# One decoder layer on one core: x's rows loaded earlier, one convolution tap and one gate block given to VectorE, and two sums with their low parts last

## The chip, the cores and the metric

The kernel runs as one program on one core of a Trainium2 chip. A core has TensorE (PE, matrix products into PSUM), VectorE (DVE), ScalarE (ACT), GpSimd (POOL) and a sync engine (SP) whose queue here issues nearly all DMA transfers between HBM and the on-chip memory SBUF. Each engine works through its own list of instructions in order, and waits on semaphores for the others. The metric is the device time of one execution in microseconds (us), the median of several runs.

## The reference

One layer of a hybrid decoder for 1024 tokens with 1024 channels, all in float32. Cut to what matters:

```python
h = rms_norm(x, attn_norm_w)
q, k, v, u, g = split(h @ w_in)                # 1024, 1024, 1024, 2048, 2048 columns
# branch A: differential attention, 8 heads, causal, T5 relative bias
a = softmax(q1 k1 * scale + bias) v - lam * softmax(q2 k2 * scale + bias) v   # per head, q and k RMS-normed
y_a = (rms_norm(a, subln_w) * (1 - lam_init)) @ w_proj_attn
# branch B: gated causal depthwise convolution of width 31
c = causal_depthwise_conv(u_a * sigmoid(u_b), conv_w) + conv_b
y_b = silu(layer_norm(c)) @ w_proj_conv
g_a, g_b = split(sigmoid(g + gate_b))
x = x + (g_a * y_a + g_b * y_b) @ w_out
h = rms_norm(x, ffn_norm_w)
x = x + (silu(h @ w_gate) * (h @ w_up)) @ w_down
```

## The kernel before, in words

**Numbers.** Every matrix operand is split in two: a high part, which ScalarE makes by a cast (`split_hi`, line 120), and a low part, the remainder, which VectorE (`split_lo`, line 125) or in the first stage GpSimd (`low`, line 131) makes by a subtraction. A product is then three matmuls into the same PSUM bank, `mm3` at lines 168 to 170: high by high, then one low part, then the other. Names in the profile follow that: `whi`/`wlo` are a weight's two parts, `hT_hi`/`hT_lo` those of the normalised input, `ph`/`pl` those of the softmax weights, `vh`/`vl` of the values, `aTh`/`aTl` of attention's output, `mTh`/`mTl` of the merge.

**Stages**, in order of time in the profile: an opening that loads and normalises x (to about 60 us); most of the input projection with the convolution's input u (to about 300 us); attention (to about 815 us); the two output projections and the gated merge (to about 1000 us); the product with `w_out` (to about 1070 us); the channel mixer with its gate, up and down products (to the end). Three of the products are done as seven half-size block products in place of eight (lines 438 to 448), with sums of blocks as operands; the block names "11", "12", "S1" to "S4", "22" stand for those.

**Attention.** `steps` (line 1413) lists 64 steps, one per head and row block. In each step `scores` does the score products (lines 1315 and 1316, into one of three banks `sc`), VectorE adds the bias and takes the minimum (line 1317, which frees the bank), ScalarE the exponential (1322), VectorE the combination of the two softmaxes (1332). One step later `turn` transposes the result on PE (1354, bank `pT`), ScalarE and VectorE copy it as `ph` and `pl`. Then `weigh` (lines 1359 to 1369) multiplies with the values into a bank `pW`, ScalarE copies that to `ar` (1368), and `back` transposes `ar` (1374, bank `pB`). Row blocks of the last head, 7, run in the order 6, 7, 4, 5, 2, 3, 0, 1, so the last weighting of all is `(H - 1, 0)`, with two k-steps.

Between these steps PE gets filler from a generator, `fill`: for each head the projection to q and k (`q_item`, lines 815 to 870: four passes of `gemm_N` per pair of row blocks, into banks `pg`), and the 32 blocks of the gate projection (`g_item`, lines 639 to 646: one `gemm_T` of 24 matmuls with 512 columns, then ScalarE adds the gate's bias at line 644 and the SP queue stores the block). `gemm_N` (line 381) takes eight k-steps: four on each of two weight halves, each of them a pair `whi`, `wlo`.

VectorE's own filler is the depthwise convolution, `conv_taps` (585 to 614): per channel block of 128 channels one first tap on ScalarE (line 593: input times weight plus bias into `acc`), then thirty taps on VectorE (line 599), and a store of the channel to `c_d` (605), which GpSimd's queue adds to a sum `cs_d` (583). For the last four channel blocks `acc` is a single buffer in SBUF, so the first tap of one block waits until the store of the block before it has landed.

**The end of attention** (lines 1494 to 1543): `group()` takes one more gate block from `fill`, the last `turn` follows, then `early(0)` and `early(1)` load finished heads, another `group()` takes the last gate block but one, the last weighting is done, and heads 0 to 4 are loaded (`early`, 1518) and split (`early_split`, 1522) for the projection that follows. The last gate block comes after that.

**The product with `w_out`** (1826 to 1900): at its start the SP queue gets loads of the weight blocks (`wload`, 1802: four of 256 KB for each block name), of the merge's block sums (`sload`, 1806) and of x's rows (`x_rows`, 1814: four of 256 KB for each quarter of x). VectorE makes the weight sums (`wless`, 1810), and adds each finished product to x's rows in place (1895), which frees the product's bank.

**Order.** The order of instructions on each engine is not the program's. A planner with a model of the machine's times picks it when the kernel is built. What the program pins: `with after(ins):` puts each instruction made inside the block behind `ins` on the engine of `ins`; `last_of(engine)` is the last instruction of that engine that the program has made so far; `in_order()` pins all three compute engines.

Of the kernel before, what the change touches and what calls it, by code (L numbers as in the profile page):

```python
# [16 lines left out]
P = 128  # L17
# [40 lines left out]
def kernel(  # L58
# [108 lines left out]
    def mm3(o, lh, ll, rh, rl, start, stop):  # L167
        pe.matmul(o, lh, rh, start=start, stop=False)  # L168
        pe.matmul(o, lh, rl, start=False, stop=False)  # L169
        last_mm[0] = pe.matmul(o, ll, rh, start=False, stop=stop).ins  # L170
# [86 lines left out]
    def pcol(key, k=0):  # L257
        c = col[key] + k
        return pvec[:, c : c + 1]
# [121 lines left out]
    def gemm_N(o, halves, shi, slo, i):  # L381

        ts = slice(i * P, (i + 1) * P)
        for k in range(NKT):
            whi, wlo = halves[k // 4]
            mm3(o, kt(shi, k)[:, ts], kt(slo, k)[:, ts], whi[:, k % 4, :], wlo[:, k % 4, :], k == 0, k == NKT - 1)


    v_hi = [dr.tile([S, 256], F32, name=f"v_hi{j}") for j in range(4)]
    v_lo = [dr.tile([S, 256], F32, name=f"v_lo{j}") for j in range(4)]  # L390
# [194 lines left out]
    def conv_taps(c):  # L585
        acc = []

        def first_tap():
            if c < CONV_PSUM:
                acc.append(pcv[0].tile([P, S], F32, tag="acc", name=f"acc{c}", bufs=1))  # L590
            else:
                acc.append(cv.tile([P, S], F32, tag="acc", name=f"acc{c}", bufs=1))
            act.activation(acc[0][:], us[c][:], AF.Identity, bias=pcol("conv_b", c), scale=cw[:, c, CW - 1 : CW])  # L593

        def tap(t):
            def go():
                n = CW - 1 - t
                a_ = acc[0][:, n:]
                dve.scalar_tensor_tensor(a_, us[c][:, : S - n], cw[:, c, t : t + 1], a_, op0=ALU.mult, op1=ALU.add)  # L599
                if t == 0:  # L600
                    if c < CONV_PSUM:
                        done = cv.tile([P, S], F32, tag="acc", name=f"done{c}", bufs=1)
                        act.copy(done[:], acc[0][:])
                        acc[0] = done
                    nc.sync.dma_start(c_d[c][:], acc[0][:])
                    if c == 0:
                        nc.sync.dma_start(cs_d[:], acc[0][:])
                if c > 1 and t == CW // 2:
                    with after(last_of(mybir.EngineType.DVE)):
                        add_tile(c - 1)  # L610

            return go

        return [first_tap] + [tap(t) for t in range(CW - 2, -1, -1)]
# [19 lines left out]
    def u_item(c):  # L634
        w = ws.next(), ws.next()
        for sb in range(2):
            yield from u_half(c, w, sb)

    def g_item(c):
        w = ws.next()  # L640
        for sb in range(2):
            o = gemm_T(w, hT_hi, hT_lo, sb)
            sg = wp.tile([P, 512], F32, tag="sg", name=nm("sgg"), bufs=2)
            act.activation(sg[:], o[:], AF.Identity, bias=pcol("gate_b", c))
            nc.sync.dma_start(g_d[c][:, sb * 512 : (sb + 1) * 512], sg[:])
            yield


# [166 lines left out]
    def q_item(h):  # L815
        halves = [ws.next(), ws.next()]
        t = {}
        T[h] = t
        for b in (1, 0):
            raw = qkp.tile([P, 4, 256], F32, tag="qkraw", name=nm("qkraw"), bufs=2)  # L820
            ss = sm.tile([P, 16], F32, tag="ss16", name=nm("ss16"))
            for i2 in range(2):
                o = pg()
                for e in range(2):
                    gemm_N(o[:, 256 * e : 256 * (e + 1)], halves, hT_hi, hT_lo, 4 * b + 2 * i2 + e)
                act.copy(raw[:, 2 * i2 : 2 * i2 + 2, :], o[:].rearrange("p (e c) -> p e c", c=256))
                q_squares(raw, ss, (2 * i2, 2 * i2 + 1))
                if i2 == 0:
                    yield
            r = rstd_of(ss[:], 16, 1.0 / HD, fast=h > 0)  # L830
            r4 = raw[:].rearrange("p i (g d) -> p (i g) d", d=HD)
            dve.tensor_tensor(r4, r4, r.unsqueeze(2).to_broadcast([P, 16, HD]), op=ALU.mult)

            def turn_qk(z, key, b, raw):


                dma = nc.sync.dma_start
                pt = pm("pQ")
                for i in range(4):
                    pe.transpose(pt[:, i * P : (i + 1) * P], raw[:, i, z * P : (z + 1) * P], ident[:])  # L840
                w = pcol(key + "n")

                def part(j):
                    return qkp.tile([P, 512], F32R, tag=f"{key}s{j}", name=f"{key}s{j}_{h}_{b}", bufs=2 if key == "q" else 3)

                s1, s2 = part(1), part(2)
                act.activation(s1[:], pt[:], AF.Identity, scale=w)
                lo = part(3) if key == "q" else qkp.tile([P, 512], F32R, tag="klo", name=f"klo_{h}_{b}", bufs=1)
                dve.scalar_tensor_tensor(lo[:], pt[:], w, f32(s1[:]), op0=ALU.mult, op1=ALU.subtract)
                if key == "q":  # L850
                    dma(f32(s2[HD:, :]), f32(s1[HD:, :]))
                    lo2 = part(4)
                    for one, two in ((s1, s2), (lo, lo2)):
                        if one is lo:
                            dma(f32(two[HD:, :]), f32(one[HD:, :]))
                        dma(f32(two[:HD, :]), f32(one[HD:, :]))
                        dma(f32(one[HD:, :]), f32(one[:HD, :]))
                    t["q", b] = (s1, lo), (s2, lo2)
                else:
                    act.activation(s2[HD:, :], pt[HD:, :], AF.Identity, scale=w[HD:, :])  # L860
                    dma(f32(s2[:HD, :]), f32(lo[HD:, :]))
                    dma(f32(s1[HD:, :]), f32(lo[:HD, :]))
                    t["k", b] = s1, s2

            for z, key in ((1, "k"), (0, "q")):
                free = NT * (h - 1) + (0 if key == "k" and b else NT if key == "q" and not b else NT // 2)
                late.append((free if h else 0, lambda a_=(z, key, b, raw): turn_qk(*a_)))
            yield  # L870
# [467 lines left out]
    def turn(h, i):  # L1338

        b = i // 2  # L1340
        if (h, b) not in PT:
            ph = aps.tile([P, NT, 256], F32R, tag="ph", name=nm("ph"), bufs=1)
            pl = aps.tile([P, NT, 256], F32R, tag="pl", name=nm("pl"), bufs=1)
            pool.memset(f32(ph[:, 2 * b + 1, 0:P]), 0.0)
            pool.memset(f32(pl[:, 2 * b + 1, 0:P]), 0.0)
            PT[h, b] = ph, pl
        ph, pl = PT[h, b]
        e = ES.pop((h, i))
        qs = slice((i % 2) * P, (i % 2 + 1) * P)
        for k0 in range(0, i + 1, 4):  # L1350
            n = min(4, i + 1 - k0)
            pt = pm("pT")
            for k in range(n):
                pe.transpose(pt[:, k * P : (k + 1) * P], e[:, (k0 + k) * P : (k0 + k + 1) * P], ident[:])  # L1354
            src = pt[:, : n * P].rearrange("p (k q) -> p k q", q=P)
            split_hi(ph[:, k0 : k0 + n, qs], src)
            split_lo(pl[:, k0 : k0 + n, qs], src, ph[:, k0 : k0 + n, qs])

    def weigh(h, b):

        ph, pl = PT.pop((h, b))
        vh, vl = V[h]
        o = pm("pW")
        nkt = 2 * b + 2
        for k in range(nkt):
            mm3(o[:, :256], vh[:, k, :], vl[:, k, :], ph[:, k, :], pl[:, k, :], k == 0, k == nkt - 1)
        ar = aps.tile([P, 256], F32, tag="ar", name=nm("ar"), bufs=1)
        act.copy(ar[:], o[:, :256])
        return ar
# [124 lines left out]
    n = len(steps)  # L1494
    group()
    turn(*steps[-1])
    bg.until(0)
    add_tile(NKT - 1)
    qk_ctx.close()
# [16 lines left out]
    def early(h):  # L1516
        loaded[h] = aps.tile([P, S], F32, tag="E", name=f"early{h}", bufs=4)
        nc.sync.dma_start(loaded[h][:], a_d[h][:])
# [5 lines left out]

    early(0)
    early(1)
    group()
    weighs.append((n, steps[-1][:1] + (steps[-1][1] // 2,)))
    slot(n, len(late))
    early(2)  # L1530
# [295 lines left out]
    for z, (z_, b_, s_, (l, c), full) in enumerate(WSEVEN):  # L1826
        if z == 0:
            with after(last_of(mybir.EngineType.SP)):
                wload("12", (1, 0))
                x_rows(0, 0)  # L1830
                wload("S3", (0, 1))
                wload("S1", (0, 0))
                wload("S4", (1, 1))
                sload("S2")
                x_rows(1, 1)
                x_rows(0, 1)
                sload("S4")
                sload("S3")
                x_rows(1, 0)
# [328 lines left out]
```

## Time and profile before

| | |
|---|---|
| median of 3 runs | 1724.55 us (1723.59 to 1724.76) |
| the profiled execution's own time | 1723.72 us |
| its span, first to last instruction | 1721.9 us |
| TensorE's granted clock | full in all 40 slices |
| busy: VectorE, ScalarE, GpSimd | 74%, 51%, 13% of the span |
| bytes moved by DMA | 281.66 MB, 164 GB/s in the mean |

In the rows that follow, times are us from the span's start. A row of the timeline has the start, the duration, the engine, the line of the kernel, the operation, what it writes and reads, the shapes and the number of merged instructions; in brackets stands how long the engine was idle just before, and who released it. "SPq" is the SP queue, where an instruction issues a DMA. A row of the chain has start, duration and the link. Matmuls are pipelined, and their ends are modelled: the distance between two starts is the better measure of PE's pace.

### The profile page before, as it was taken

The numbers are of one execution on the slowest core, as the hardware profiler recorded it, in microseconds if no ns is written. First come the engines' busy times: TensorE is split into PE (matmuls) and PEld (weight loads), VectorE is DVE, ScalarE is ACT, GpSimd is POOL, SyncE is SP. The second block draws the span as 40 slices with busy tenths as digits, with TensorE's granted clock in tenths as the row PEclk, the third lists the DMA queues.
The fourth block names the chain that finished last, engine by engine and source line by source line (L and its number), as shares of the span: only waits on it lengthen the run. The fifth ranks groups of instructions, "written<-read, shape, count | busy, mean of one in ns | idle before, by whom it ended". The sixth has DMA issues, their size and how long they took to land.

```text
span 1721.9 us, 25846 instructions
## 1 busy us (share of the span) xinstructions
PE 1709.5 (99%) x9237; PEld 1477.1 (86%) x9237; DVE 1277.4 (74%) x2127; ACT 870.9 (51%) x1958; POOL 227.0 (13%) x216
## 2 busy tenths in 40 slices
PE   8999999999999999999999999999999999999999
PEld 7998889998998998988888878888888888888887
DVE  7676888899888987977677769966766666575544
ACT  5334335777776786866466325633333333333332
POOL 5997851000000000000000000000000000000000
PEclk9999999999999999999999999999999999999999
DMA  6333555346345344354873683244455445597663
GB/s 207 116 122 121 154 143 158 106 120 176 94 125 165 94 125 141 100 152 139 309 237 129 202 302 102 80 141 153 153 172 166 153 145 165 176 369 271 216 217 128
DMA packets 261859, 281.66 MB, mean 164 GB/s; under 512 B 17023, under 2 KB 182480, under 8 KB 261730
## 3 DMA queue, kind: packets, MB, share of 16 engines
q1 hardware_dynamic: 253632, 266.70, 48.0%
q0 software_dynamic: 6464, 10.41, 2.8%
q10 hardware_dynamic: 1634, 2.89, 0.5%
q8 instruction: 73, 1.20, 0.3%
q14 instruction: 56, 0.46, 0.1%
HBM read 181.84 MB, written 85.50 MB: 155 GB/s over the span
## 4 chain that ended last, share of the span: by engine, by line
PE 95%; DMA 2%; DVE 1%; ACT 1%; issue 0%; POOL 0%; SPq 0%; DVEq 0%; ACTq 0%
PE acc L1005 30%; PE pg L169 13%; PE pg L170 13%; PE pg L168 13%; PE acc L493 12%; PE wo L1883 3%; PE sc L1316 2%; PE sc L1315 2%; PE pT L1354 2%; PE pg L1131 1%; PE pW L168 1%; PE pW L169 1%; PE pW L170 1%; PE pQ L840 1%; DMA room<-in_w_out_dram 1%
## 5 line engine op out<-in xcount | busy, mean ns | idle before, releaser
L599 DVE SCALAR_TENSOR_TENSOR acc<-u,cw,acc 128x1023 f32<-128x1023 f32 (+14 forms) x240 | 303.6, 1265 | 19.2 <-ACT acc L593 16.7
L170 PE MATMUL pg<-whi,hT_lo 128*128 128x256 f32 x704 | 200.7, 285 | 0.0
L169 PE MATMUL pg<-wlo,hT_hi 128*128 128x256 f32 x704 | 199.8, 284 | 0.7 <-POOL wlo L131 0.7
L168 PE MATMUL pg<-whi,hT_hi 128*128 128x256 f32 x704 | 199.0, 284 | 0.0
L125 DVE TENSOR_TENSOR wlo<-draw,whi 128x1024 fp32r<-128x1024 f32 x75 | 91.8, 1224 | 86.3 <-ACT whi L120 79.5
L120 ACT CAST whi<-draw 128x1024 fp32r<-128x1024 f32 x75 | 79.1, 1055 | 129.5 <-PE acc L493 116.0
L169 PEld LDWEIGHTS pg<-wlo,hT_hi 128*128 128x128 f32 x704 | 134.1, 191 | 3.0 <-POOL wlo L131 0.9
L168 PEld LDWEIGHTS pg<-whi,hT_hi 128*128 128x128 f32 x704 | 133.8, 191 | 1.9
L170 PEld LDWEIGHTS pg<-whi,hT_lo 128*128 128x128 f32 x704 | 134.1, 190 | 1.5
L120 ACT CAST whi<-wraw 128x1024 fp32r<-128x1024 f32 x90 | 94.6, 1052 | 60.5 <-PE pg L169 27.1
L493 PE MATMUL acc<-wlo,whi 128*128 128x512 f32 x308 | 119.8, 389 | 0.0
L493 PE MATMUL acc<-whi,wlo 128*128 128x512 f32 x308 | 119.8, 389 | 0.0
L168 PE MATMUL pg<-hT_hi,whi 128*128 128x512 f32 x288 | 115.0, 399 | 0.0
L169 PE MATMUL pg<-hT_lo,whi 128*128 128x512 f32 x288 | 114.0, 396 | 0.0
L170 PE MATMUL pg<-hT_hi,wlo 128*128 128x512 f32 x288 | 113.7, 395 | 0.0
L1322 ACT ACTIVATE E<-E,mn 128x640 f32<-128x640 f32 (+7 forms) x128 | 99.3, 776 | 20.8 <-DVE mn L1317 20.6
L120 ACT CAST whi<-s 128x1024 fp32r<-128x1024 f32 x54 | 56.8, 1052 | 95.9 <-PE acc L1005 92.6
L125 DVE TENSOR_TENSOR wlo<-wraw,whi 128x1024 fp32r<-128x1024 f32 x75 | 94.3, 1260 | 14.5 <-ACT whi L120 14.3
L1005 PE MATMUL acc<-h_lo,whi 128*128 128x512 f32 x240 | 93.4, 389 | 0.0
L1005 PE MATMUL acc<-h_hi,whi 128*128 128x512 f32 x240 | 93.4, 389 | 0.0
L1317 DVE CUSTOM_DVE_ANT_0 E<-sc,tb 128x512 f32<-128x512 f32 (+3 forms) x128 | 74.5, 586 | 21.7 <-PE pT L1354 12.4
L1005 PE MATMUL acc<-h_hi,wlo 128*128 128x512 f32 x240 | 90.1, 389 | 0.0
(379 smaller groups left out, 4599.0 us busy)
## 6 DMA issues: line engine op xcount, KB each, us to landing
wraw<-in_w_gate_up_dram SPq DMA_DIRECT2D x44, 512.0 KB, 4.8
wraw<-in_w_in_dram SPq DMA_DIRECT2D x38, 512.0 KB, 4.0
qs<-qs SPq DMA_DIRECT2D x96, 128.0 KB, 2.3
wd<-in_w_down_dram SPq DMA_DIRECT2D x44, 256.0 KB, 3.1
tdT<-wd SPq DMA_DIRECT2D x88, 128.0 KB, 4.7
draw<-sdS SPq DMA_DIRECT2D x44, 256.0 KB, 4.2
draw<-tdT SPq DMA_DIRECT2D x44, 256.0 KB, 3.2
wraw<-in_w_in_dram SPq DMA_DIRECT2D x32, 256.0 KB, 3.2
```

The source lines that it names most:

```text
L120: act.copy(dst, src)
L125: last_lo[0] = dve.tensor_tensor(dst, src, f32(hi), op=ALU.subtract).ins
L168: pe.matmul(o, lh, rh, start=start, stop=False)
L169: pe.matmul(o, lh, rl, start=False, stop=False)
L170: last_mm[0] = pe.matmul(o, ll, rh, start=False, stop=stop).ins
L493: m = pe.matmul(o[s_][i][:], l_[:, ts], r_[:, 512:], start=start and j + y_ == 0, stop=j == n - 1 and y_ == 2, skip_group_check=not start,)
L599: dve.scalar_tensor_tensor(a_, us[c][:, : S - n], cw[:, c, t : t + 1], a_, op0=ALU.mult, op1=ALU.add)
L1005: last_mm[0] = pe.matmul(o[:], a_[x_][:, k, :], b_[y_][:, k, :], start=start and k + x_ + y_ == 0, stop=k == 3 and x_ == 1, skip_group_che ...
L1315: pe.matmul(o[:, :w], qh[:, qs], k, start=True, stop=False)
L1317: dve.tensor_tensor_reduce(e[:, ks], o[:, :w], tb[:, S - nk + c0 : S - nk + c0 + w], 1.0, mn[:, j : j + 1] if c0 else 3.0e38, ALU.add, ALU ...
L1322: act.activation(e[:, :nk], e[:, :nk], AF.Exp, bias=mn[:, j : j + 1], scale=-1.0, accum_out=l[:, j : j + 1])
L1883: last_mm[0] = pe.matmul(o[s_][i][:], A[u_], B[v_], start=start and j + y_ == 0, stop=j == 3 and y_ == 2, skip_group_check=not start,).ins
```

## The change

Five edits:

1. The first tap of the last channel block (channel 7) is a `tensor_scalar` on VectorE (multiply by the weight, add the bias) in place of ScalarE's activation.
2. For head 1, the first product of its second row half (`(h, b, i2, e) == (1, 1, 0, 0)`) uses `gemm_N_lows_last`: the first weight half as before; for the second half the eight matmuls on the weight's high part first, then the four on its low part.
3. The last weighting, head 7 and block 0, multiplies `ph` with `vh` and `vl` for both k-steps first, and `pl` with `vh` last.
4. The gate block taken by the second `group()` is kept back, and then emptied by VectorE in place of ScalarE, behind the last `turn`'s last instructions on VectorE and ScalarE.
5. In the SP queue, x's first quarter of rows is pinned behind the loads of "12", "S3" and "S1", and the loads of "S4", "S2" and all that follows are pinned behind those rows.

```diff
+    def gemm_N_lows_last(o, halves, shi, slo, i):
+
+        ts = slice(i * P, (i + 1) * P)
+        for k in range(NKT // 2):
+            mm3(o, kt(shi, k)[:, ts], kt(slo, k)[:, ts], halves[0][0][:, k, :], halves[0][1][:, k, :], k == 0, False)
+        for k in range(NKT // 2, NKT):
+            w = halves[1][0][:, k % 4, :]
+            pe.matmul(o, kt(shi, k)[:, ts], w, start=False, stop=False)
+            pe.matmul(o, kt(slo, k)[:, ts], w, start=False, stop=False)
+        for k in range(NKT // 2, NKT):
+            last_mm[0] = pe.matmul(
+                o, kt(shi, k)[:, ts], halves[1][1][:, k % 4, :], start=False, stop=k == NKT - 1
+            ).ins
...
-            act.activation(acc[0][:], us[c][:], AF.Identity, bias=pcol("conv_b", c), scale=cw[:, c, CW - 1 : CW])
+            if c == NKT - 1:
+                dve.tensor_scalar(
+                    acc[0][:], us[c][:], cw[:, c, CW - 1 : CW], pcol("conv_b", c), op0=ALU.mult, op1=ALU.add
+                )
+            else:
+                act.activation(acc[0][:], us[c][:], AF.Identity, bias=pcol("conv_b", c), scale=cw[:, c, CW - 1 : CW])
...
+    kept = [None]
+
     def g_item(c):
...
-            act.activation(sg[:], o[:], AF.Identity, bias=pcol("gate_b", c))
-            nc.sync.dma_start(g_d[c][:, sb * 512 : (sb + 1) * 512], sg[:])
+            def out(sg=sg, o=o, sb=sb):
+                if kept[0] is None:
+                    act.activation(sg[:], o[:], AF.Identity, bias=pcol("gate_b", c))
+                else:
+                    dve.tensor_scalar(sg[:], o[:], pcol("gate_b", c), None, op0=ALU.add)
+                nc.sync.dma_start(g_d[c][:, sb * 512 : (sb + 1) * 512], sg[:])
+
+            if kept[0] is None:
+                out()
+            else:
+                kept[0].append(out)
             yield
...
-                    gemm_N(o[:, 256 * e : 256 * (e + 1)], halves, hT_hi, hT_lo, 4 * b + 2 * i2 + e)
+                    gemm = gemm_N_lows_last if (h, b, i2, e) == (1, 1, 0, 0) else gemm_N
+                    gemm(o[:, 256 * e : 256 * (e + 1)], halves, hT_hi, hT_lo, 4 * b + 2 * i2 + e)
...
-        for k in range(nkt):
-            mm3(o[:, :256], vh[:, k, :], vl[:, k, :], ph[:, k, :], pl[:, k, :], k == 0, k == nkt - 1)
+        if (h, b) == (H - 1, 0):
+            for k in range(nkt):
+                pe.matmul(o[:, :256], vh[:, k, :], ph[:, k, :], start=k == 0, stop=False)
+                pe.matmul(o[:, :256], vl[:, k, :], ph[:, k, :], start=False, stop=False)
+            for k in range(nkt):
+                last_mm[0] = pe.matmul(
+                    o[:, :256], vh[:, k, :], pl[:, k, :], start=False, stop=k == nkt - 1
+                ).ins
+        else:
+            for k in range(nkt):
+                mm3(o[:, :256], vh[:, k, :], vl[:, k, :], ph[:, k, :], pl[:, k, :], k == 0, k == nkt - 1)
...
     turn(*steps[-1])
+    turned = last_lo[0], last_of(mybir.EngineType.Activation)
     bg.until(0)
...
     early(1)
+    kept[0] = []
     group()
+    with after(turned[0]), after(turned[1]):
+        kept[0].pop()()
+    kept[0] = None
...
                 wload("12", (1, 0))
-                x_rows(0, 0)
                 wload("S3", (0, 1))
                 wload("S1", (0, 0))
+            with after(last_of(mybir.EngineType.SP)):
+                x_rows(0, 0)
+            with after(last_of(mybir.EngineType.SP)):
                 wload("S4", (1, 1))
                 sload("S2")
                 x_rows(1, 1)
```

## The prediction

> **What bounds the kernel now.** I read the page first (busy shares, chain), then PE's waits, then PE's rows around each wait, then the other engines' rows at the same places.
>
> ```profile
> span 1721.9 us, 25846 instructions
> PE 1709.5 (99%) x9237; PEld 1477.1 (86%) x9237; DVE 1277.4 (74%) x2127; ACT 870.9 (51%) x1958; POOL 227.0 (13%) x216
> ...
> PE 95%; DMA 2%; DVE 1%; ACT 1%; issue 0%; POOL 0%; SPq 0%; DVEq 0%; ACTq 0%
> ```
>
> TensorE (PE) is busy for 99% of the span and carries 95% of the chain that ended last. No part of the change removes a matmul: the two re-orderings only change in which order the same products go in. So what can be won is the time in which PE stands still, and it stands still seldom. From PE's own rows, in order of time:
>
> ```profile
> 296.26 0.28 PE L170 MATMUL pg<-whi,hT_lo 128*128 128x256 f32 x1
> 296.38 0.28 PE L168 MATMUL pg<-whi,hT_hi 128*128 128x256 f32 x1
> 297.32 0.39 PE L169 MATMUL pg<-wlo,hT_hi 128*128 128x256 f32 x1 [0.66 <-POOL wlo L131]
> ...
> 687.61 0.28 PE L169 MATMUL pg<-wlo,hT_hi 128*128 128x256 f32 x1
> 688.45 0.44 PE L1374 MATMUL pB<-ident,ar 128*128 128x128 f32 x2 [0.56 <-ACT ar L1368]
> ...
> 810.98 0.38 PE L1354 MATMUL pT<-ident,E 128*128 128x128 f32 x2
> 811.20 0.38 PE L1374 MATMUL pB<-ident,ar 128*128 128x128 f32 x2
> 812.18 0.39 PE L168 MATMUL pW<-ph,vh 128*128 128x256 f32 x1 [0.60 <-ACT ph L120]
> ...
> 813.33 0.40 PE L168 MATMUL pg<-hT_hi,whi 128*128 128x512 f32 x1
> ...
> 821.53 0.39 PE L170 MATMUL pg<-aTh,wlo 128*128 128x512 f32 x1
> 822.28 0.51 PE L168 MATMUL pg<-aTh,whi 128*128 128x512 f32 x1 [0.36 <-ACT aTh L120]
> ...
> 1020.69 0.39 PE L1883 MATMUL wo<-wlo,mTh 128*128 128x512 f32 x1
> 1020.92 0.39 PE L1883 MATMUL wo<-whi,mTl 128*128 128x512 f32 x1
> 1022.09 0.47 PE L1883 MATMUL wo<-whi,mTh 128*128 128x512 f32 x1 [0.78 <-DVE xa L1895]
> ```
>
> Durations of matmuls overlap, so I read starts. A 256-column product starts 0.12 us after the one before it (296.26, 296.38), a 512-column one 0.23 us (1020.69, 1020.92), two transposes take 0.22 (810.98, 811.20). What is over that is lost: 0.94 - 0.12 = 0.82 us at 296 (place A, released by GpSimd's low part of a weight); 0.84 - 0.12 = 0.72 us at 687 (B, ScalarE's copy "ar"); at 811 (C) two transposes and six 256-column products would need 0.22 + 0.72, and 811.20 to 813.33 is 2.13, so 1.19 us; 0.75 - 0.23 = 0.52 us at 821 (D), where the next product waits again; 1.17 - 0.23 = 0.94 us at 1021 (F, VectorE's add of x's rows). The change aims at A, B, C and F: 0.82 + 0.72 + 1.19 + 0.94 = 3.67 us, 0.21% of the span. That is the ceiling but for D. The question is how much of each survives.
>
> **A: low parts last in head 1's first q/k product.** The eight k-steps use two weight halves. PE stops at the fifth, whose second product wants the low part of half two.
>
> ```profile
> 294.87 2.39 POOL L131 TENSOR_TENSOR wlo<-wraw,whi 128x1024 fp32r<-128x1024 f32 x1 [19.02 <-ACT whi L120]
> 307.58 1.24 ACT L593 ACTIVATE acc<-u,pvec,cw 128x1024 f32<-128x1024 f32 x1 [2.60 <-DMA c_d<-done]
> 308.86 1.28 DVE L599 SCALAR_TENSOR_TENSOR acc<-u,cw,acc 128x1023 f32<-128x1023 f32 x1 [1.75 <-ACT acc L593]
> 310.06 0.48 DVE L1317 CUSTOM_DVE_ANT_0 E<-sc,tb,mn 128x256 f32<-128x256 f32 x1
> 311.19 0.40 PE L1315 MATMUL sc<-ks,qs 128*128 128x512 f32 x1
> ...
> 689.37 0.68 DVE L1317 CUSTOM_DVE_ANT_0 E<-sc,tb 128x512 f32<-128x512 f32 x1
> 690.14 0.31 PE L1315 MATMUL sc<-ks,qs 128*128 128x128 f32 x1
> ```
>
> GpSimd ends at 294.87 + 2.39 = 297.26. With the change, eight products on the high part go first: from 296.38 to 296.38 + 8 x 0.12 = 297.34. The wait is gone, 0.82 us. No instruction is added and no DMA moves. What is late next: VectorE. Its convolution taps restart at 308.86 behind ScalarE's first tap, which started at 307.58 when a DMA of the finished channel landed, and neither hangs on the stalled product. The score product at 311.19 uses a bank that VectorE's row of 310.06 frees at 310.54, so 0.65 us are free there. Such a handover itself takes about 0.09: at 690.14 PE takes a bank that VectorE freed at 689.37 + 0.68 = 690.05. So 0.65 - 0.09 = 0.56 us pass. Bounds 0.56 and 0.82; I take 0.6, near the lower, since the row that limits it is there.
>
> **B: the last channel's first tap moves from ScalarE to VectorE.**
>
> ```profile
> 681.18 0.42 DVE L125 TENSOR_TENSOR pl<-pT,ph 128x256 fp32r<-128x256 f32 x1 [0.69 <-ACT ph L120]
> 684.33 0.28 PE L169 MATMUL pW<-pl,vh 128*128 128x256 f32 x1
> 686.90 1.24 ACT L593 ACTIVATE acc<-u,pvec,cw 128x1024 f32<-128x1024 f32 x1 [3.70 <-DMA c_d<-acc]
> 688.17 1.28 DVE L599 SCALAR_TENSOR_TENSOR acc<-u,cw,acc 128x1023 f32<-128x1023 f32 x1 [4.94 <-ACT acc L593]
> ...
> L1779 DVE TENSOR_SCALAR fnw_b<-fnw_b x1: 694/694/694, 942.2 to 942.2; 128x1024 f32<-128x1024 f32 x1
> ```
>
> ScalarE stands 3.70 us in front of the tap until the store of channel 6 has landed, then computes 1.24 us; "ar" and PE's transposes queue behind it. Without the tap ScalarE copies "ar" as soon as PE's weighting, under way at 684.33, has ended, and the 0.72 us at 688.45 go. VectorE loses nothing by the wait: it idles 4.94 us for the same tap already. But it now computes it. The row nearest in kind is a multiply of 128x1024 f32 with constants, SBUF to SBUF: 694 ns; the dearest plausible is a two-tensor pass of the size, the tap's own 1.28. With 0.69 VectorE's second tap starts near 686.9 + 0.69 = 687.6 instead of 688.17, 0.6 us earlier, less than PE's 0.72. This matters, for the score product at 690.14 starts 0.09 us after its bank is free: PE can come forward here only as far as VectorE does. So 0.6 us at 694 ns, and 0.09 or nothing at 1.28. I take 0.6. The Trainium skill ("VectorE: DVE Perf Modes", section "The perf-mode tier table (the rule you actually need)") says that a tensor_scalar on fp32 in SBUF runs at two elements a cycle and a two-tensor operation at one; the 694 ns against 1.28 us agree. By it the sum keeps its 0.6; had scalars read per partition no part in that rule, it would lose 0.5. In this trace no operation of this form with two per-partition scalars stands.
>
> **C and D: the gate block before the last, and head 7's last weighting.**
>
> ```profile
> 811.18 0.69 ACT L644 ACTIVATE sgg<-pg,pvec 128x512 f32<-128x512 f32 x1
> 811.77 0.36 ACT L120 CAST ph<-pT 128x256 fp32r<-128x256 f32 x1
> 812.16 0.42 DVE L125 TENSOR_TENSOR pl<-pT,ph 128x256 fp32r<-128x256 f32 x1 [0.69 <-ACT ph L120]
> ...
> 811.39 7.00 DMA early<-a_d
> 818.42 1.05 ACT aTh L120
> ...
> 821.16 1.06 ACT aTh L120
> ```
>
> ScalarE empties the gate block (0.69 us) just ahead of the high part that PE wants. With the change that emptying goes to VectorE behind its last low part (812.16). The transposes of 810.98 end at 811.36; the high part can start between then and 811.77. I take 811.56, 0.2 us earlier. Then PE does its four high products from about 811.97, the low part ends 0.2 us earlier at 812.38, and the last two follow without a wait: 811.97 + 0.72 = 812.69 instead of 813.33, 0.64 us. The emptying on VectorE costs about what it did on ScalarE (VectorE's pass over 128x512 out of PSUM at 689.37 took 0.68) and nothing that PE waits for is queued behind it: VectorE's next work, the low parts of the loaded heads waits for ScalarE's conversions in any case. Its store leaves the SP queue about 1 us later, behind the load of 811.39.
>
> But PE's next stop, D, does not move with it. The chain goes from the transposes at 811.36 through a load of 7.00 us (landed 818.39), then ScalarE's conversions one after the other to 822.22. That load starts when the transposes have read the buffer, ahead of everything that C changes. PE arrives 0.64 us sooner and waits 0.64 us longer. So C and D together: nothing at the one end, 0.64 us if ScalarE's order lets the pieces before 821.16 slip forward, 0.64 + 0.52 if D closes too. I take nothing, by the chain's own rows. A's and B's gains pass, since the load is issued behind PE's transposes.
>
> **F: x's rows ahead of four weight loads and S2.**
>
> ```profile
> 1004.72 0.54 SPq L555 DMA_DIRECT2D soS<-gt  x1
> 1006.47 3.76 SPq L1802 DMA_DIRECT2D room<-in_w_out_dram  x6
> 1012.52 2.26 SPq L1814 DMA_DIRECT2D xa<-in_x_dram  x4
> 1017.73 0.69 DVE L1895 TENSOR_TENSOR xa<-wo,xa 128x512 f32<-128x512 f32 x1 [3.35 <-DMA xa<-in_x_dram]
> 1023.65 2.49 DVE L1810 TENSOR_TENSOR room<-room,room 128x512 f32<-128x512 f32 x4
> ```
>
> Four row loads move past the four loads of S4 (the last four of the six at 1006.47) and three of S2: seven of 256 KB. The SP queue issues one each 3.76 / 6 = 0.63 us there, so the first row leaves 7 x 0.63 = 4.4 us earlier, near 1008, if the buffer is free. The rows' tiles lie where the merge's last tiles were, whose last store left at 1004.72; a load takes about 5.2 us here (1012.52 to 1017.7), so the row may have to wait for about 1010. That is the bound on the other side: 2.5 us earlier. Either way VectorE's first add starts by 1015.2 instead of 1017.73. PE's stop is 0.94 us behind a run of adds that began 3.35 us late for this load, so 2.5 us are enough, and the whole 0.94 goes. What is pushed back: S4 and S2 by four row loads and up to 2.3 us of a held SP queue. If the rows leave from 1010 on, S4's last load leaves 8 x 0.63 = 5 us behind, near 1015, and lands 5.2 us later, near 1020. Its first reader is VectorE's difference at 1023.65. So 3.4 us of cover are left; were it gone, each further microsecond would cost PE one.
>
> **Sum.** 0.6 + 0.6 + 0 + 0.94 = 2.1 us. The profiled run took 1723.72 us, 1.8 us outside its span; less 2.1 gives 1721.6. The median of the three runs shown is 0.83 us above it, 1724.55, so the forecast is 1722.4. I call 0.2% (3.45 us) what a measurement of this kernel can just tell from no change.
>
> **Rivals.** *All four gains survive*: 0.82 + 0.72 + 0.64 + 0.94 = 3.1 us, with D closed 3.6, so 1720.9 to 1721.4. For it speaks that the order on each engine is planned anew; against it the two handovers of 0.65 and 0.09 us. Chance 0.2. *The gains are eaten*: each shift is paid back at the next VectorE handover, or the tap takes 1.28 us, or other instructions are re-ordered by the planner to equal loss; only F or less remains, 0 to 1.2 us, time 1723.3 to 1724.6 or a little more. Chance 0.17. *The tap blocks VectorE* (the other side): VectorE takes its instructions in order. The tap cannot start before 686.9. If the planner, which counts on an earlier landing, puts it ahead of the low part of 681.18, that low part ends near 687.6 + 0.42 = 688.0 instead of 681.60, and PE's product that reads it, at 684.33 now, waits to about 688.1: 3.8 us lost, less B's 0.72, so with A and F kept 3.8 - 0.7 - 0.6 - 0.9 = +1.6 us, 1726.1; without them 1727.6. It decides the sign once PE loses more than 0.72 + 0.6 + 0.94 = 2.3 us there. Against it: the tap is tied behind the step's last VectorE instruction. Chance 0.1. The Trainium skill ("TensorE: Matmul & The Clock Gate", section "Architectural detail: the array is 16× 32×32, not 1× 128×128") states that VectorE's and ScalarE's queues are strictly first in, first out; ScalarE's 3.70 us before its tap, with "ar" behind it, agree. The likeliest case, 0.53, lies within 1721.4 to 1723.2 itself.
>
> **How the numbers follow.** The range takes the main case, most of the survivors and of the eaten gains: 1720.4 to 1725.3, leaving out the blocked tap and the far end of a closed D. Faster by over 0.2% needs 3.45 us, the best part of the first rival and some luck elsewhere: 0.17. Slower by over 0.2% needs the blocked tap without the other gains, or a re-planned stage that I don't see: 0.09. The rest, 0.74, is within.
>
> **What would show it.** Right: PE's rows near 296, 688 and 1021 at full cadence; the tap on VectorE near 0.69 us at 687; the row loads issued between 1007 and 1010; PE's stop before 822 longer than 0.52 us. Wrong: a VectorE row before the tap that idles with low parts queued behind it; a new PE stop behind a score bank near 311 or 690 larger than 0.3 us; the SP queue standing at the row loads past 1011 with the weights of S4 late; or stops at places that this text doesn't name.

## The result, and the profile after

| | kernel before | changed kernel |
|---|---|---|
| median | 1723.59 us (19 runs, 1722.29 to 1726.66) | 1720.22 us (19 runs, 1718.71 to 1720.87) |
| ratio, 95% interval | 1 | 0.9979 [0.9973, 0.9985] |
| span of the profiled execution | 1721.9 us | 1717.7 us |

The change makes the kernel 3.4 us faster, just over 0.2%. The forecast was 1722.4 us, so 2.2 us too slow. Of that, 0.96 us is the starting point: the three runs shown beforehand had a median of 1724.55, and over 19 runs the kernel before has 1723.59. The other 1.3 us is the gain: 3.4 in place of 2.1.

The page of the changed kernel (busy shares, then the chain by engine):

```profile
span 1717.7 us, 25841 instructions
PE 1709.4 (100%) x9237; PEld 1478.4 (86%) x9237; DVE 1280.5 (75%) x2129; ACT 868.8 (51%) x1956; POOL 227.1 (13%) x216
...
PE 98%; DMA 1%; ACT 0%; DVE 0%; issue 0%; DVEq 0%
```

PE does the same 9237 matmuls in the same 1709 us, and it now carries 98% of the chain, up from 95%. Only its standstills went. PE's rows at the same products as before:

```profile
296.57 0.28 PE L396 MATMUL pg<-whi,hT_lo 128*128 128x256 f32 x1
296.70 0.74 PE L398 MATMUL pg<-wlo,hT_hi 128*128 128x256 f32 x4
297.28 0.28 PE L168 MATMUL pg<-whi,hT_hi 128*128 128x256 f32 x1
...
809.09 0.44 PE L1414 MATMUL pB<-ident,ar 128*128 128x128 f32 x2
809.67 0.36 PE L1398 MATMUL pW<-ph,vh 128*128 128x256 f32 x1
...
810.22 0.40 PE L1401 MATMUL pW<-pl,vh 128*128 128x256 f32 x2
810.46 0.40 PE L168 MATMUL pg<-hT_hi,whi 128*128 128x512 f32 x1
...
818.70 0.39 PE L170 MATMUL pg<-aTh,wlo 128*128 128x512 f32 x1
819.46 0.50 PE L168 MATMUL pg<-aTh,whi 128*128 128x512 f32 x1 [0.37 <-ACT sgg L667]
...
1017.57 0.39 PE L1930 MATMUL wo<-wlo,mTh 128*128 128x512 f32 x1
1017.79 0.39 PE L1930 MATMUL wo<-whi,mTl 128*128 128x512 f32 x1
1018.02 0.39 PE L1930 MATMUL wo<-whi,mTh 128*128 128x512 f32 x1
```

A (296) and F (the three products that stood around 1020.69 to 1022.09 now start at 1017.57 to 1018.02) run at full cadence, and no stop above 0.12 us is left between 297 and 808 us, so B is gone too. C is down to 0.60 us (0.30 of it just ahead of the first row at 809). D is 0.76 - 0.23 = 0.53 us, and its releaser is another: not the conversion of head 4 ("aTh") but the emptying of a gate block ("sgg"). ScalarE's rows there:

```profile
815.96 1.06 ACT L120 CAST aTh<-early 128x1024 fp32r<-128x1024 f32 x1 [0.29 <-DMA early<-a_d]
...
817.77 1.06 ACT L120 CAST whi<-wraw 128x1024 fp32r<-128x1024 f32 x1
818.70 0.70 ACT L667 ACTIVATE sgg<-pg,pvec 128x512 f32<-128x512 f32 x1
...
819.90 1.05 ACT L120 CAST aTh<-early 128x1024 fp32r<-128x1024 f32 x1
```

And the same rows of the kernel before:

```profile
818.42 1.05 ACT L120 CAST aTh<-early 128x1024 fp32r<-128x1024 f32 x1 [0.20 <-DMA early<-a_d]
...
820.23 1.06 ACT L120 CAST whi<-wraw 128x1024 fp32r<-128x1024 f32 x1
821.16 1.06 ACT L120 CAST aTh<-early 128x1024 fp32r<-128x1024 f32 x1
822.11 0.70 ACT L644 ACTIVATE sgg<-pg,pvec 128x512 f32<-128x512 f32 x1
```

The order is another: the planner now lets ScalarE empty the last gate block before it converts head 4. No line of the diff asks for that. At F the row loads leave at 1005.74 and the first add starts at 1010.18:

```profile
1005.74 1.76 SPq L1859 DMA_DIRECT2D xa<-in_x_dram  x4
...
1010.18 0.69 DVE L1942 TENSOR_TENSOR xa<-wo,xa 128x512 f32<-128x512 f32 x1 [0.50 <-DMA xa<-in_x_dram]
```

### The profile page after: what moved, and what is told of

The parts are those of the page before. It is cut to its first block, busy times and chain, and to the rows that moved or that the text cites. A ratio compares the mean times of both kernels' runs of the same rounds, so it can differ in the third digit from the quotient of the medians.

```text
span 1717.7 us, 25841 instructions
## 1 busy us (share of the span) xinstructions
PE 1709.4 (100%) x9237; PEld 1478.4 (86%) x9237; DVE 1280.5 (75%) x2129; ACT 868.8 (51%) x1956; POOL 227.1 (13%) x216
## 4 chain that ended last, share of the span: by engine, by line
PE 98%; DMA 1%; ACT 0%; DVE 0%; issue 0%; DVEq 0%
PE acc L1036 30%; PE pg L168 13%; PE pg L169 13%; PE pg L170 13%; PE acc L507 12%; PE wo L1930 4%; PE sc L1347 2%; PE sc L1346 2%; PE pT L1385 2%; PE pg L1162 1%; PE pW L168 1%; PE pW L170 1%; PE pW L169 1%; PE pQ L871 1%; PE tr L1817 0%; PE pS L1435 0%
```

## The experiments

PE's stops, read as in the prediction from the distances between starts, for every profiled run (us; stops under 0.12 left out, so C of before is 1.10 here and 1.19 in the prediction). "688" is the place of B, "793" a place where the kernel before does not stop; D is every stop near 821, whatever released it. The last column is the median less that of the kernel before on the same chip (both over all their executions); for the runs with one execution it is that one time less the median.

| run | A | 688 | 793 | C | D | F | sum | time - before |
|---|---|---|---|---|---|---|---|---|
| before | 0.82 | 0.72 | 0 | 1.10 | 0.89 | 0.94 | 4.47 | 0 |
| changed | 0 | 0 | 0 | 0.60 | 0.53 | 0 | 1.13 | -3.37 |
| e13, changed again | 0 | 0 | 0 | 0.60 | 0.73 | 0 | 1.33 | -3.34 |
| e1, C alone | 0.81 | 0.63 | 0 | 0.40 | 0.73 | 0.64 | 3.21 | -1.09 |
| e3, gate block alone | 0.81 | 1.03 | 0 | 0.75 | 1.23 | 0.25 | 4.07 | -0.6 |
| e7, order at D alone | 0.82 | 1.23 | 0 | 1.10 | 0.57 | 0.86 | 4.58 | +0.4 |
| e2, changed without C | 0 | 0 | 0 | 0.80 | 0.86 | 0 | 1.66 | -2.69 |
| e4, changed, pin at D | 0 | 0 | 0 | 0.60 | 0.28 | 0 | 0.88 | -3.5 |
| e5, A alone | 0 | 0 | 0.82 | 0.80 | 0.75 | 1.11 | 3.48 | +0.8 |
| e6, B alone | 0.83 | 1.54 | 0 | 0.80 | 0 | 0.66 | 3.83 | +0.9 |
| e9, changed without B | 0 | 0 | 0.82 | 0.60 | 1.21 | 0 | 2.63 | -2.38 |
| e10, changed without A | 0.83 | 0.90 | 0 | 0.60 | 0 | 0 | 2.33 | -2.05 |
| e12, changed, slow tap | 0 | 0 | 0 | 0 | 1.14 | 0 | 1.14 | -3.63 |
| e11, F alone | 0.82 | 1.06 | 0 | 1.11 | 0.77 | 0 | 3.76 | -0.68 |
| e8, changed, other pin | 0 | 0 | 0 | 0.60 | 0 | 0 | 0.60 | -3.56 |
| e14, the same again | 0 | 0 | 0 | 0.60 | 0 | 0 | 0.60 | -4.13 |

For the ten runs that were timed in several executions, 4.47 less the sum of stops and the measured gain agree within 0.6 us, so the stops are the account to read. Left out of the table are a stop of 0.27 us near 998 that all have, 0.34 us at 311 in e6 and 0.21 us at 834 in e5, and stops of 0 to 0.8 us near 137 and 204 us; these last and the opening, which differs by up to 1.2 us, come and go in kernels with and without the edits. This is why a single time says little here.

**C and D.** First, edits 3 and 4 alone on the kernel before:

> The kernel before with only the third and fourth edit (low parts last in head 7's last weighting, gate block emptied by VectorE). Theory R, the prediction's: what PE wins at C it waits for again at D, so C's loss falls from 1.19 to about 0.6 us, D's grows from 0.88 to about 1.5, and the time stays within 0.3 us of before. Theory O, formed on the changed kernel's trace: the planner now lets ScalarE empty the last gate block ahead of head 4's conversion (1.05 us), so D's chain from the landed load is about 1 us shorter: C falls to 0.6, D to 0.5, and the time falls by 0.9 to 1.0 us, to about 1722.6.

1722.14 us against 1723.23, ratio 0.9993 [0.9984, 1.0002]; C 0.40, D 0.73, together 1.13 in place of 1.99. Theory O, by its stops; the time agrees but its interval reaches 1. The chain's length is the thing to read, in ScalarE's and PE's rows of this run:

```profile
810.01 0.38 PE L1408 MATMUL pB<-ident,ar 128*128 128x128 f32 x2
...
817.22 1.05 ACT L120 CAST aTh<-early 128x1024 fp32r<-128x1024 f32 x1 [0.20 <-DMA early<-a_d]
...
819.96 0.70 ACT L662 ACTIVATE sgg<-pg,pvec 128x512 f32<-128x512 f32 x1
...
820.71 0.50 PE L168 MATMUL pg<-aTh,whi 128*128 128x512 f32 x1 [0.40 <-ACT sgg L662]
```

From PE's transposes "pB" to the landing of head 3's load it takes 817.22 - 810.01 = 7.21 us; before, 818.42 - 811.20 = 7.22. From the landing to PE's restart at D it takes 3.5 us; before, 822.87 - 818.42 = 4.45 (PE's second product in that stop starts at 822.87, as "sgg" ends at 822.81). The one difference is ScalarE's conversion of head 4, 1.05 us, which moved behind the emptying. The gate block's edit alone, without that new order:

> The kernel before with the fourth edit alone (gate block emptied by VectorE); the order of all else is that of before, at D too. Both R and O: PE reaches D 0.4 to 0.6 us earlier, finds the same chain (landing, conversions, emptying) and waits that much longer: C about 0.6 to 0.8, D 1.3 to 1.5, their sum as before, 2.1 us. Theory G (C's gain reaches the end): D stays at 0.9 and the sum falls to 1.6.

```profile
810.85 0.38 PE L1399 MATMUL pB<-ident,ar 128*128 128x128 f32 x2
811.48 0.38 PE L168 MATMUL pW<-ph,vh 128*128 128x256 f32 x1 [0.24 <-ACT ph L120]
...
818.10 1.06 ACT L120 CAST aTh<-early 128x1024 fp32r<-128x1024 f32 x1 [0.22 <-DMA early<-a_d]
...
821.79 0.70 ACT L662 ACTIVATE sgg<-pg,pvec 128x512 f32<-128x512 f32 x1
...
821.95 1.09 PE L168 MATMUL pg<-aTh,whi 128*128 128x512 f32 x2 [0.70 <-ACT aTh L120]
```

C falls by 0.35 us (1.10 to 0.75), D grows by 0.34 (0.89 to 1.23): 1.98 in all, 1.99 before. From landing to the second product's start (822.54) again 4.45 us. So with the old order, what PE wins at C it waits for at D, to a hundredth. The order alone, without any edit, is the counterpart (head 4's conversion pinned behind the emptying):

```diff
-    for h in range(2, 5):
+    for h in range(2, 4):
         early_split(h)
...
     with after(m):
         for _ in fill:
             pass
+    with after(last_of(mybir.EngineType.Activation)):
+        early_split(4)
```

> The kernel before with none of the five edits, but with head 4's conversion pinned behind ScalarE's emptying of the last gate block. Theory O: C stays at 1.1 us; at D the bank is free one conversion earlier, PE goes on 3.5 us behind the landing of head 3 in place of 4.5, so D's 0.88 us fall to 0.0 to 0.2 and the sum C + D from 2.0 to 1.1 to 1.3 us, without any of the edits. Rival: what sets D is something that the edits moved, and D stays at 0.7 to 0.9.

```profile
818.64 1.05 ACT L120 CAST aTh<-early 128x1024 fp32r<-128x1024 f32 x1 [0.20 <-DMA early<-a_d]
...
822.14 0.50 PE L168 MATMUL pg<-aTh,whi 128*128 128x512 f32 x1 [0.40 <-ACT sgg L644]
```

C stays at 1.10, D falls from 0.89 to 0.57, less than expected, because the load took 7.54 us in this run (7.00 before). From landing (818.64) to restart (822.14) it is 3.50 us as expected. Theory O holds in the chain's length, and it missed the size of the stop, which the landing sets too. The changed kernel without edits 3 and 4:

> The changed kernel without the third and fourth edit; ScalarE's new order at D (emptying ahead of head 4's conversion) stays. Theory G (C's own gain reaches the end): C's loss is back at 1.19 us, D stays at 0.5, so 0.6 us slower than the changed kernel, about 1720.8. Theory O (D's chain decides, C only moves the place of the wait): C at 1.19, D closed to under 0.1, and the time within 0.2 us of the changed kernel, about 1720.3.

1720.54 us, ratio 0.9981 [0.9972, 0.9990]: 0.7 us less gain than the changed kernel (-2.69 against -3.37). C is 0.80 and not 1.19, since the new plan already puts the emptying ahead of the weighting; D is 0.86 where theory O wanted none. Landing to restart is 3.50 us again, but the loads leave later. SP's rows, first of this run, then of the changed kernel:

```profile
808.40 0.81 SPq L664 DMA_DIRECT2D g_d<-sgg  x1
809.30 4.85 SPq L1538 DMA_DIRECT2D early<-a_d  x3
```

```profile
807.49 2.14 SPq L1559 DMA_DIRECT2D early<-a_d  x3
810.62 0.32 SPq L670 DMA_DIRECT2D g_d<-sgg  x1
```

With the gate block emptied later, its store leaves behind two of the loads and not ahead of them. Head 3's load leaves at 809.18 in the changed kernel and at 809.90 here. (Its duration says nothing: 6.76 us there, 7.03 here, but 7.06 in e13, which is the changed kernel again.) That is the second thing that edits 3 and 4 do, though only against this plan: in the kernel before, the store left behind head 3's load too, at 811.89 against 811.39. The last of this group pins the old order into the changed kernel:

```diff
-    m = last_mm[0]
+    m, fifth = last_mm[0], last_of(mybir.EngineType.Activation)
...
-    with after(m):
+    with after(m), after(fifth):
```

> The changed kernel with one pin more: ScalarE empties the last gate block behind head 4's conversion, as in the kernel before. Theory O: D grows from 0.53 to about 1.4 us and everything behind it comes 0.9 us later. Theory G: D is set by what PE reaches, the order of two ScalarE instructions matters by under 0.3 us: D at 0.5 to 0.8.

Neither: D fell to 0.28 us. The pin did put the emptying last on ScalarE (at 821.10), but the planner also re-ordered the products of four banks on PE, and the first that needs this bank now comes 27 products later. It isn't the clean test that it was meant to be; it shows that the plan around a pin moves with it.

**A and B.** Each alone on the kernel before:

> The kernel before with the second edit alone (low parts last in head 1's q/k product). The stop near 296 us, 0.82 us, goes. Record: a score bank near 311 us that VectorE frees lets only 0.56 to 0.6 us pass, the rest comes back as a new PE stop of 0.2 to 0.25 us there. Rival: attention's instructions are planned anew behind the product, no stop over 0.12 us appears between 297 and 330 us, and 0.8 us pass.

> The kernel before with the first edit alone (channel 7's first tap on VectorE). The stop near 688 us, 0.6 to 0.7 us, goes. Record: the tap starts only near 686.9 us, when the store of channel 6 lands, takes 0.69 us, and the score bank at 690 us lets 0.6 us pass. Rival, from the changed kernel's trace: the store leaves and lands some 5 us earlier, the tap starts near 681 us and takes 0.81 us, and no stop over 0.12 us is left between 680 and 700 us.

A's stop is gone in e5, and no stop stands between 297 and 330 us: the rival. The score bank's slack is still there (0.61 us, 0.65 before; 0.68 in the changed kernel). PE does not arrive there earlier, because the plan gives it 104 matmuls between the end of that product and the score product where it did 97: 7 x 0.12 = 0.84 us of work from later on. In other plans the bank does limit: e9 has 0.33 us of slack there, and in e6 PE stops for 0.34. But two more things moved, 390 us behind the edit: B's stop is gone without B's edit, and near 793 us there are two new ones of 0.82 in all. VectorE finishes channel 6 earlier in the new plan, and its store leaves ahead of the gate block's store and a weight load. Before (SP's queue, the first tap stands in the prediction at 686.90), then the changed kernel, where the tap is VectorE's:

```profile
679.15 0.58 SPq L645 DMA_DIRECT2D g_d<-sgg  x1
679.78 0.45 SPq L306 DMA_DIRECT2D wraw<-in_w_in_dram  x1
680.27 0.69 SPq L605 DMA_DIRECT2D c_d<-acc  x1
```

```profile
677.83 0.58 SPq L624 DMA_DIRECT2D c_d<-acc  x1
678.50 0.39 SPq L925 DMA_DIRECT2D tb<-t_d  x1
678.95 0.80 SPq L670 DMA_DIRECT2D g_d<-sgg  x1
...
681.34 0.81 DVE L608 TENSOR_SCALAR acc<-u,cw,pvec 128x1024 f32<-128x1024 f32 x1 [0.55 <-DMA c_d<-acc]
```

The store leaves 2.4 us earlier and is done 3.5 us after its issue, not 6.6, so the tap starts at 681.34 and not 686.90. With B alone the plan ahead of it is the old one, and the tap on VectorE gains nothing:

```profile
688.62 0.81 DVE L608 TENSOR_SCALAR acc<-u,cw,pvec 128x1024 f32<-128x1024 f32 x1 [4.53 <-DMA c_d<-acc]
...
690.67 0.68 DVE L1336 CUSTOM_DVE_ANT_0 E<-sc,tb 128x512 f32<-128x512 f32 x1
...
691.41 0.33 PE L1334 MATMUL sc<-ks,qs 128*128 128x128 f32 x1 [1.38 <-DVE mn L1336]
```

VectorE stands 4.53 us for the store, with the score bank's work queued behind tap one and two; PE stops 1.54 us at the bank. The stop is larger than in the five runs that have the tap on ScalarE in the old order (0.63 to 1.23 us in before, e1, e3, e7 and e11), but the tap's engine is not what made it so. PE's 4472nd matmul, the score product of 690.14 in the kernel before, starts 3.25 us behind the tap in those five runs, 3.24 in e6 and 3.25 in e10, which also has the tap on VectorE. What differs is the landing: counted from a matmul 200 places earlier, the tap starts after 27.93 to 28.53 us in the five, 28.89 in e6 and 28.25 in e10, and the stop goes with that. The score product itself does start sooner behind the tap, 2.79 us (691.41 - 688.62) and not 3.24 (690.14 - 686.90), since VectorE's tap is shorter; but it stands three matmuls earlier in PE's list here, so PE has that much less done. That is the prediction's rival of the eaten gains, not that of the tap that blocks VectorE: the low part that it named runs ahead of the tap, at 682.04. Next, the changed kernel without B, and without A:

> The changed kernel with channel 7's first tap back on ScalarE. Theory P (A's edit makes the planner store channel 6 earlier, so the tap's data are there 5 us sooner and its engine does not matter): no stop at 688 us, but the stop of 0.8 us at 793 us that the run with A alone showed, since the order from 680 us on is that of A alone; 0.6 to 0.9 us slower than the changed kernel, about 1721.0. Theory R (record): the stop at 688 us is back with 0.6 to 0.7 us, nothing new at 793.

1720.98 us, ratio 0.9985 [0.9976, 0.9994], 1.0 us less gain. No stop at 688, the two at 793 are back (0.56 and 0.26): theory P for the place. D grows too, from 0.53 to 1.21 us, which neither theory had; 0.63 of it is a wait for the low part of a head by VectorE. PE's rows there:

```profile
792.00 0.27 PE L1342 MATMUL sc<-ks,qs 128*128 128x128 f32 x1
792.68 0.39 PE L1341 MATMUL sc<-ks,qs 128*128 128x256 f32 x1 [0.40 <-DVE mn L1343]
```

So in the changed kernel B's edit earns its place not at 688, where A's re-planning has already closed the stop, but because the plan behind it no longer has the late score banks at 793, and has the shorter D.

> The changed kernel without the second edit (head 1's product as before). Theory R (record, parts add up): only the stop of 0.82 us at 296 is back, about 1721.1. Theory P: the order of attention is the old one, channel 6 is stored late, and the tap on VectorE holds up the score bank near 690 us by 1.0 to 1.6 us: with the 0.82 us at 296 some 2 us slower than the changed kernel, about 1722.3, near the kernel before.

1721.31 us, ratio 0.9988 [0.9979, 0.9996], 1.3 us less gain. A's 0.83 is back and 0.90 at the score bank near 690, again with VectorE idle for 3.90 us ahead of the tap: theory P's order, with a stop just under its size. In time it falls between the two, nearer to theory R, since D is 0 in this plan. The last one asks whether the tap's length mattered:

```diff
-                dve.tensor_scalar(
-                    acc[0][:], us[c][:], cw[:, c, CW - 1 : CW], pcol("conv_b", c), op0=ALU.mult, op1=ALU.add
-                )
+                dve.scalar_tensor_tensor(
+                    acc[0][:], us[c][:], cw[:, c, CW - 1 : CW], pcol("conv_b", c).to_broadcast([P, S]),
+                    op0=ALU.mult, op1=ALU.add,
+                )
```

> The changed kernel with channel 7's first tap as a two-operand form on VectorE (the bias spread along the row as second operand), expected to take 1.28 us in place of 0.81. Theory R (record): the tap's length passes to the score bank, 0.5 us are lost. Theory P: VectorE stands 1.2 us behind the second tap for a bias table's load, so 0.47 us more cost nothing; same time as the changed kernel, 1720.2, unless the planner orders the rest differently, which PE's stops would show.

```profile
682.58 1.28 DVE L608 SCALAR_TENSOR_TENSOR acc<-u,cw,pvec 128x1024 f32<-128x1024 f32 x1 [0.53 <-DMA c_d<-acc]
685.71 0.69 DVE L1349 CUSTOM_DVE_ANT_0 E<-sc,tb 128x512 f32<-128x512 f32 x1 [1.85 <-DMA tb<-t_d]
```

1719.73 us, ratio 0.9981 [0.9972, 0.9990]: no loss, no stop near 688. VectorE idles 1.85 us behind the slow tap for a bias table. The plan from here on differs: C is 0 and D 1.14, in all about the changed kernel's 1.13. That the two sums agree is chance, for D has other releasers here: VectorE's low parts of two heads, 0.70 and 0.44 us, not the emptying.

**F.**

> The kernel before with the fifth edit alone (x's rows ahead of the loads of S4 and S2). All theories: PE's stop near 1021 us, 0.25 to 1.1 us in the runs with the old order, goes to under 0.1; row loads leave some 5 us sooner; nothing else changes but the order of two VectorE rows; 0.7 us faster, about 1722.7. If S4's loads are now late, a PE stop of 0.2 us or more behind 1023 us.

```profile
1009.10 1.76 SPq L1828 DMA_DIRECT2D xa<-in_x_dram  x4
```

1722.68 us, ratio 0.9992 [0.9983, 1.0000], a gain of 0.68 whose interval ends at none. The stop is gone and none follows it. The row loads leave 3.4 us sooner, not 5: the SP queue stands 2.0 us ahead of them until the merge's last store ("soS") has landed. The size of the stop without the edit was 0.94, 0.64, 0.25, 0.86, 1.11 and 0.66 in six profiles, 0.74 in the mean: PE's stop ended 4.36 us behind the start of VectorE's first add in all six, while the loads came at other times against PE's own work.

**A shorter chain at D.** On the changed kernel, a weight's high part, which PE reads only behind all products shown here, is pinned behind the emptying:

```diff
+    emptied = last_of(mybir.EngineType.Activation)
     inatt[0] = False
...
-    w3 = [ws.next()]
+    with after(emptied):
+        w3 = [ws.next()]
```

In the two traces PE's and the SP queue's instructions stand in the same order.

> The changed kernel with one pin more: ScalarE makes the high part of a weight that is needed only later (1.06 us) behind the emptying of the last gate block, not ahead of it. Theory O: the bank is free near 818.5 us, ahead of PE, which comes at 818.9; D falls from 0.53 to under 0.1 us, and the time by 0.4 to 0.5 us against the changed kernel, to about 1719.8. Rival: the next link of the chain (head 3's low part by VectorE) takes the place, D stays above 0.3.

1719.34 us, ratio 0.9982 [0.9972, 0.9992], D gone, nothing in its place. Beside each other on one chip:

> The changed kernel once more, as the partner of the next run on the same chip. Theory O: PE goes on after D 3.5 us behind the landing of head 3's load, whenever that is; D between 0 and 1.2 us as the landing falls, time near 1720.2.

> The changed kernel with the pin of the earlier run (the emptying of the last gate block ahead of a weight's high part). Theory O: PE goes on 2.5 us behind the landing, one cast sooner, so D stays under 0.1 us even where the load lands late; 0.4 to 0.8 us faster than the changed kernel beside it. Theory P: what is won at D is waited for again behind it, the two agree within 0.2 us.

1720.14 us (0.9983 [0.9974, 0.9992]) and 1719.35 us (0.9976 [0.9967, 0.9985]). Landing to restart is 3.50 us in e13, to the hundredth as in the changed kernel's first profile, with the landing 0.4 us later and D 0.2 us longer. ScalarE in e14:

```profile
817.48 1.05 ACT L120 CAST aTh<-early 128x1024 fp32r<-128x1024 f32 x1 [0.24 <-DMA early<-a_d]
...
819.28 0.70 ACT L667 ACTIVATE sgg<-pg,pvec 128x512 f32<-128x512 f32 x1
819.85 1.06 ACT L120 CAST whi<-wraw 128x1024 fp32r<-128x1024 f32 x1
```

The bank is free 2.5 us behind the landing, at 819.98, and PE takes it at 820.40 without a stop; 3.50 us behind the landing would have been 820.98. (The load lands 1.1 us later than in e13, but PE is later by as much, from the opening on.) D is on the path to the end: 0.8 us between the medians, 0.73 by the stops. The two intervals overlap, so by time alone the gain over the changed kernel is likely and not shown; e14's median is the lowest of all but that of its own first run (1719.34).

## Why the prediction was wrong, step by step

- **What bounds the kernel: right.** PE's standstills are the account, and the stops' sums follow the times within 0.6 us.
- **C and D "nothing": the step that failed.** The term measured 0.86 us in stops (0.66 with the profile of e13), of the 1.2 us by which the sum was short. Its mechanism was right, and e3 shows it to a hundredth: with ScalarE's order as it was, C gives 0.35 and D takes 0.34. What failed was to take that order as given. The text named the condition ("0.64 us if ScalarE's order lets the pieces before 821.16 slip forward") and then priced it at nothing "by the chain's own rows", though the kernel's order is planned anew at every build. The planner moved head 4's conversion behind the emptying, and the chain from landing to restart went from 4.45 to 3.50 us (before, e3 and e11 against changed, e1, e2, e7, e9 and e13). The same move came with edits of A or B alone. Of the planner's reasons nothing was measured.
- **A, taken at 0.6: too low, and for a reason that was not there.** All 0.82 us went. The handover at the score bank was real (0.61 us of slack in e5, 0.68 in the changed kernel) but did not limit there, since the plan put 7 more matmuls ahead of it. A was worth more than its stop: by re-planning what follows it also closed B's, and leaving A out cost 1.3 us (e10).
- **B, taken at 0.6: the result near, the way wrong.** "The tap cannot start before 686.9" held only in the old plan; in the new one it starts at 681.34. The tap takes 0.81 us, not 0.69, and e12 shows that even 1.28 would not have mattered there. With the old plan B's edit gains nothing (stops of 1.54 us in e6 and 0.90 in e10, 0.63 to 1.23 without it, each as its store landed), so the handover of 0.09 us that the prediction quoted was the right thing to fear: VectorE as the bound behind a late store. In the changed kernel leaving B out costs 1.0 us; its stops are 0.82 us at 793 and 0.68 at D.
- **F, taken at 0.94: right in mechanism, a little high.** One profile's stop stood for a quantity that varies between 0.25 and 1.11; the mean is 0.74 and the time 0.68. The hold that the prediction reckoned with was there: the queue stood 1.9 us for the store, until 1005.74. PE is 3.1 us ahead of the kernel before at this place, so that is 1008.9 on its times, within 1007 to 1010; in e11 it is 1009.10. The first add came 4.2 us sooner in e11 (1013.48), near the bound without a hold. S4 and S2 were in time.
- **The rule on VectorE's rate: agrees in order, not in size.** The Trainium skill ("VectorE: DVE Perf Modes", section "The perf-mode tier table (the rule you actually need)") has a `tensor_scalar` on fp32 in SBUF at twice the rate of a `tensor_tensor`. With two scalars per partition the tap took 0.81 us against 1.28 for the two-operand form, a `scalar_tensor_tensor`: 1.6 times.
- **The sum.** Measured in stops, before to changed: A 0.82, B 0.72, C and D 0.86, F 0.94, together 3.34; by time 3.37. That lies between the two ends of the rival "all four survive", 3.1 us and, with D closed, 3.6; but B's stop went by another road, and D closed only in part. The range ended 0.2 us above the result: the baseline of three runs was 0.96 us high and was not widened for, and without that the error in C and D would have stayed inside the range.

## What to carry to other kernels

Where a planner orders the instructions, an edit's effect is its own stop and the plan that it triggers: read which waits in the old trace come from order alone (here one conversion ahead of the instruction that PE waits for) and give a chance to each being re-ordered, in both directions. Gains from several edits need not add up then: run each alone and each left out, and account by PE's stops, which resolve 0.1 us where the times resolve about 1. When a stop is a chain of "landing, then engine X's list", the cheapest move is to take out of that list what nobody waits for.

## What the runs showed of the hardware

- A 512 KB store to HBM was done 3.5 us after its issue when it left ahead of a 256 KB store and a 512 KB load, and 6.6 to 7.0 us after it (before, e6, e10) when it left behind them on the same queue. Which of the two delays it was not measured apart.
- A `tensor_scalar` on VectorE over 128x1024 f32 in SBUF takes 0.81 us with two scalars read per partition, 0.69 with one constant and one operation (line 1779 of the kernel before); the form with the bias spread as a second operand takes 1.28.
- Two profiles of one kernel differ by 0.4 us of span (the changed kernel, 1717.7 and 1718.1) and 0.9 us (e8 and e14, 1717.6 and 1718.5). In the first pair it is 0.29 us at 137 us and 0.20 at D; in the second the opening is 1.0 us longer (PE's 100th matmul starts at 24.0 and 25.0 us) and two stops, 0.46 us at 137 and 0.42 at 204, change places. The chains of the stops at 137 (e5) and 204 us (e14) go back to a weight's load; what lengthens the opening was not followed.
